# S5 stage of a hybrid decoder: the input factor moved from W to C, W of all quarters and K ahead of the scan

## The chip, the cores and the metric

One core of one Trainium2 chip. The time is the device time of one execution, in microseconds (us). The engines are TensorE (PE in the profile, PEld its weight loads), VectorE (DVE), ScalarE (ACT), GpSimd (POOL) and SyncE (SP), which here issues most DMAs. Each runs its own list of instructions, and they wait for one another through semaphores.

## What is computed

A trunk of two layers on x of 256 tokens by 2048 channels, float32. Layer 0 is an S5 mixer (a complex diagonal state-space model) and a SwiGLU feed-forward; layer 1 is dilated window attention and a second SwiGLU. The change is in the S5 mixer. Its 2048 channels are 128 groups of 16, each with 64 complex states:

```python
lb = exp((lam_re + 1j*lam_im) * dt)              # one factor for each state and group
f = (lb - 1) / (lam_re + 1j*lam_im)              # input factor
bu = einsum('bsgc,gpc->bsgp', u, f * B)          # u = rms_norm(x)
xs[s] = lb * xs[s-1] + bu[s]                     # scan over the 256 tokens
y = real(einsum('bsgp,gcp->bsgc', xs, C)) + d_skip * u
z = gelu(y);  val, gate = split(z @ w_glu);  x = x + val * sigmoid(gate)
```

f depends on state and group alone, so it may stand on B or on C: y is the same.

## The kernel before, in words

**Chunked scan.** The 256 tokens are 64 chunks of 4. Within a chunk everything is matrices: W holds f·lb^(3-j)·B for the four places j of a chunk, V (`vs`) is what each chunk adds to the state (W times u), K (`kt`, spread by DMAs into the Toeplitz blocks `th`) is what the tokens of a chunk do to y directly, and Q (`qp`) holds lb^(t+1)·C, which turns the state at a chunk's start into y. The scan proper then runs over the 64 chunk states in three levels. The groups come as 64 pairs, worked in four quarters of 16 pairs; a half is two quarters, a unit `u` is 8 pairs.

**Steps, with their lines.** `s5_params` (L253) computes lb, its powers `lam`, f (`fx`) and the factors `g` on DVE. `s5_chunk_powers` (L332, POOL) makes lb^4, lb^8 and so on. The loop at L414 scales u by the norm (POOL) and copies it with the halves of the partitions exchanged into `usw` (two SP DMAs a quarter). `w_build` (L445, DVE) makes W of a unit in 12 operations of 256 columns; `v_trans` (L458) transposes it on PE and copies it on ACT (L464); `v_build` (L468) multiplies it by u on PE and copies V on ACT (L479). `k_build` (L483) is 256 small matmuls on W and C, with copies on ACT (L498), and `t_build` (L500) its 16 SP DMAs. `q_build` (L433, POOL) makes Q of a quarter: four complex products, each of three operations on 512 columns (L235 to L237). The scan: `l1` (L532) on DVE or POOL, `l2` (L547) and `l3` (L561) on DVE; `coefs` (L542) copies the chunk powers of a half to PSUM on ACT, for DVE. `t_part` (L579) and `s_part` (L591) are the matmuls for y from th and from the states, with the gelu on ACT; `z_part` (L610) transposes the result for the GLU matmuls.

**Order.** It is written out by hand at L642 to L707, and the framework keeps it: each engine gets its instructions in the order in which the Python code issues them. W is built for units 0 to 5, with V of a unit behind it; then come K of half 0, V of units 4 and 5, Q of quarters 0 and 1 on POOL, and `l1([0, 1])`. The 24 operations of W for units 6 and 7 are strewn into `l2(0)`, V of 6 and 7 follows; `l1([3])` runs on POOL; then `l3(0)`, `s_part(0)`, and so on, with K of half 1 behind `s_part(1)`.

**The stream.** Everything after the mixer is one stream of matmul steps (`stream`, L710): a raw weight tile is loaded by SP, split into two parts (ACT and DVE) and multiplied. Its first eight steps are done unsplit (`plain`, L761; 64 matmuls in all, in blocks of 8) and are placed among the last S5 work by the calls `next(st)`; step 8 is the first ordinary one (L755 to L759). W of quarters 0 to 2 stands in the three buffers of the raw weights, W of quarter 3 in the free ends of `za` and `zb`: weights 0 to 2 can be loaded only when the last reader of that W (`v_trans`, `k_build`) is done.

Of the kernel before, what the change touches and what calls it, by code (L numbers as in the profile page):

```python
# [12 lines left out]
AF = mybir.ActivationFunctionType  # L13
# [87 lines left out]
class Trunk:  # L101
# [39 lines left out]
    def ts(self, out, in0, s1, s2, op0, op1=None):  # L141
        if op1 is None:
            self.nc.vector.tensor_scalar(out, in0, s1, None, op0)
        else:
            self.nc.vector.tensor_scalar(out, in0, s1, s2, op0, op1)
# [107 lines left out]
    def s5_params(self, rms):  # L253
# [45 lines left out]
        kv = lambda v, k: v[:, 0:128 * k].rearrange("p (k r q) -> p k r q", k=k, r=2)  # L299
        nr, fx = ps(192).rearrange("p (r q) -> p r q", r=3), ps(128).rearrange("p (r q) -> p r q", r=2)  # L300
        S3 = [128, 2, 64]
# [9 lines left out]
        nc.vector.tensor_copy(low[:, 0], lam[:, 0, 1:3])  # L311
        ts(nr[:, 0], lam[:, 0, 1], -1.0, None, add)
        ts(nr[:, 2], lam[:, 0, 1], -1.0, 1.0, mul, add)
        nc.vector.tensor_copy(nr[:, 1], lam[:, 0, 2])
        by(lam[:, 1:2, 1:3], low[:, 0], lam[:, 0:1], 1)

        u1, u2 = [v.rearrange("p (r q) -> p r q", r=2) for v in (app, az)]
        tt(u1, bc(lr, S3, [1]), nr[:, 0:2], mul)
        ts(lam[:, 1, 0], lam[:, 1, 2], -1.0, None, mul)
        nc.vector.tensor_copy(low[:, 1], lam[:, 1, 1:3])  # L320
        tt(u2, bc(li, S3, [1]), nr[:, 1:3], mul)
        tt(u1, u1, u2, add)
        by(lam[:, 2:4, 1:3], low[:, 1], lam[:, 0:2], 2)
        tt(fx, u1, bc(dens, S3, [1]), mul)
        ts(lam[:, 2:4, 0], lam[:, 2:4, 2], -1.0, None, mul)
        rms()

        g = self.g = self.bank(7).rearrange("p (j r q) -> p j r q", j=4, r=2)
        nc.vector.tensor_copy(g[:, 3], fx)
        by(g[:, 2::-1], fx, lam[:, 0:3], 3)  # L330

# [30 lines left out]
    def s5(self, st):  # L362
# [32 lines left out]
        r = self.r  # L395
        nc.scalar.activation(bt[:, 2], bt[:, 0], AF.Copy, scale=-1.0)

        def rms():
# [14 lines left out]
        next(powers)  # L413
        for k in range(4):  # L414
            qs = slice(16 * k, 16 * k + 16)
            pool.tensor_tensor(upp[:, qs, :], upp[:, qs, :], bc(rt, [128, 16, 80], [1]), mul)
            nc.sync.dma_start(usw[0:64, qs, :], upp[64:128, qs, 0:64])
            nc.sync.dma_start(usw[64:128, qs, :], upp[0:64, qs, 0:64])
        next(powers, None)
        nc.scalar.activation(ct[:, 0], ct[:, 2], AF.Copy, scale=-1.0)  # L420

# [6 lines left out]

        bq = bt.rearrange("p r (q c) -> p q r c", c=16)
        qv = [self.qp[:, k // 2, 2048 * (k % 2):2048 * (k % 2) + 2048].rearrange("p (r q m) -> p r q m", r=2, q=16)  # L430
              for k in range(4)]

        def q_build(k):  # L433

            qs = slice(16 * k, 16 * k + 16)
            sh = [128, 2, 16, 16]
            v4 = lambda v: v.rearrange("p (r q c) -> p r q c", r=2, q=16)
            for t in range(4):
                self.cmul(pool, qv[k][:, :, :, 16 * t:16 * t + 16], bc(self.lam[:, t, 1, qs], sh, [1, 3]),
                          bc(self.lam[:, t, 2, qs], sh, [1, 3]), ct[:, 1:3, qs], ct[:, 0:2, qs], v4(ptmp[0]), v4(ptmp[1]))  # L440

# [3 lines left out]
        def w_build(k, q0, n):  # L445

            qs = slice(16 * k + q0, 16 * k + q0 + n)
            sh = [128, n, 2, 16]
            w, ops = wt(k, q0, n), []
            for j in range(5):  # L450
                if j < 4:
                    ops += [lambda j=j: tt(w4(t1p[j % 2], n), bc(self.g[:, j, 0, qs], sh, [2, 2]), bq[:, qs, 0:2], mul),
                            lambda j=j: tt(w4(dtmp[j % 2], n), bc(self.g[:, j, 1, qs], sh, [2, 2]), bq[:, qs, 1:3], mul)]
                if j > 0:
                    ops.append(lambda j=j - 1: tt(w[:, :, :, j, :], w4(t1p[j % 2], n), w4(dtmp[j % 2], n), add))
            return ops
# [175 lines left out]

        ws = [self.rawtile() for _ in range(3)] + [(za[:, 3072:4096], zb[:, 3072:4096])]

        def wt(k, q0, n=1):

            w, q0 = (ws[3][q0 // 8], q0 % 8) if k == 3 else (ws[k], q0)
            return w[:, 128 * q0:128 * (q0 + n)].rearrange("p (q r j c) -> p q r j c", q=n, r=2, j=4)

        th = [tz[:, 2048 * h:2048 * h + 2048].rearrange("p (m x) -> p m x", m=4) for h in range(2)]  # L640

        for u in range(6):  # L642
            go(w_build(u // 2, 8 * (u % 2), 8))
            if u < 4:
                v_trans(u, (0, 1))
            if 0 < u < 5:
                v_build(u - 1)
        coefs(0, 5)
        k_build(0, (0, 1))
        t_build(0)  # L650
        for u in (4, 5):
            v_trans(u, (0, 0))
            v_build(u)
        q_build(0)
        q_build(1)
        next(st)
        go(l1([0, 1], dve))
        go(l2(0, self.bank(1)), w_build(3, 0, 8) + w_build(3, 8, 8))
        v_trans(6, (0, 0))
        v_build(6)  # L660
        py = [t_part(0, (1, 7))]
        v_trans(7, (0, 0))
        v_build(7)
        t1p[1] = t1p[0]
        coefs(1, 4)
        q_build(2)
        go(l1([3], pool))

        go(l3(0))
        s_part(0, py[0])  # L670
        py.append(t_part(1, (2, 3)))
        z_part(0, (1, 7), True)
        go(l3(1))
        next(st)
        s_part(1, py[1])
        k_build(1, (0, 5))
        q_build(3)
        next(st)
        t_build(1)
        next(st)  # L680
        z_part(1, (2, 3), True)
        go(l1([2], dve))
        next(st)
        next(st)
        go(l2(1, t1p[0]))
        next(st)
        py.append(t_part(2, (2, 3)))
        next(st)
        go(l3(2))
        s_part(2, py[2])  # L690
        next(st)
        go(l3(3))
# [17 lines left out]
    def stream(self, jobs):  # L710
# [50 lines left out]
        def plain(n, ms):  # L761

            jb, i = steps[n]
            k = jb["ks"][i]
            for m in ms:
                if i == 0:
                    jb.setdefault("ps", {})[m] = [self.bank(b) for b in ((1, 7), (0, 5))[m]]
                for b in range(2):
                    c = 1024 * (n % 2) + 512 * b
                    nc.tensor.matmul(jb["ps"][m][b], self.full(k // 4)[:, k % 4, 128 * m:128 * m + 128],  # L770
                                     raws[n // 2][:, c:c + 512], start=(i == 0), stop=False)
            if n % 2 == 1 and 1 in ms:
                del raws[n // 2]
                load(n // 2 + self.NRAW)

        for u in range(self.NRAW - 1):
            load(u)
        yield
        for n in range(2):
            plain(n, (0,))  # L780
        yield
        load(self.NRAW - 1)
        yield
# [402 lines left out]
```

## Time and profile before

| | us |
|---|---|
| median of 3 runs | 2210.36 (2210.22 to 2210.61) |
| the profiled execution's own time | 2210.46 |
| its span in the profile | 2208.7 |
| PE busy | 2130.2 (96%) |
| DVE busy | 1537.7 (70%) |
| ACT busy | 996.9 (45%) |
| POOL busy | 187.0 (8%) |

Times in the rows are from the start of the span. Idle time of an engine off the bounding chain costs nothing. The S5 stage ends at about 148 us, when step 8 of the stream begins.

### The profile page before, as it was taken

What the parts mean: (1) busy time and instruction counts of PE and PEld (TensorE: products, weight loads), DVE (VectorE), ACT (ScalarE), POOL (GpSimd) and SP (SyncE); (2) the same over time, 40 slices, a digit from 0 to 9 for tenths busy, and PEclk for the clock granted to TensorE, in tenths of its full rate; (3) what the DMA queues carried; (4) which work ended last, traced back from release to release, by engine and by line L of the source; (5) the groups of instructions that cost most, each with busy time, mean ns of one, the idle gap of its engine ahead of it and who ended that gap; (6) DMA issues with size and microseconds to landing.
All of it is one profiled execution on the core that took longest, in us unless ns stands there. A gap on an engine that the chain in (4) does not pass through costs nothing.

```text
span 2208.7 us, 28493 instructions
## 1 busy us (share of the span) xinstructions
PE 2130.2 (96%) x11132; PEld 1753.4 (79%) x11132; DVE 1537.7 (70%) x2656; ACT 996.9 (45%) x1147; POOL 187.0 (8%) x161
## 2 busy tenths in 40 slices
PE   3599999999999999999999999999999999999998
PEld 2468888888888888878888888878888888888886
DVE  8977777677677764756776686687767776774544
ACT  3224445444444443344445555445444444444443
POOL 6820000000000000000000000000000000000000
PEclk9699999999999999999999999999999999999999
DMA  6155555555555555455554454445555555555553
GB/s 180 52 204 191 191 191 209 191 191 191 199 188 188 197 200 192 174 205 181 210 188 150 142 189 152 137 170 191 192 209 191 188 194 190 195 211 204 191 191 133
DMA packets 66838, 404.68 MB, mean 183 GB/s; under 512 B 15248, under 2 KB 16784, under 8 KB 19088
## 3 DMA queue, kind: packets, MB, share of 16 engines
q1 hardware_dynamic: 65696, 397.12, 51.3%
q10 hardware_dynamic: 720, 4.18, 0.5%
q8 instruction: 87, 1.43, 0.3%
q0 software_dynamic: 288, 1.57, 0.2%
q14 instruction: 47, 0.39, 0.0%
HBM read 397.34 MB, written 2.10 MB: 181 GB/s over the span
## 4 chain that ended last, share of the span: by engine, by line
PE 89%; DVE 8%; issue 2%; ACT 1%; DMA 0%; ACTq 0%; DVEq 0%
PE b L756 28%; PE b L759 28%; PE b L755 28%; DVE scr L851 2%; DVE lo L139 1%; PE b L770 1%; PE b L151 1%; DVE b L139 1%; PE b L1074 1%; ACT hi L733 1%; PE b L1105 1%; DVE hi L139 1%; PE b L598 0%; DVE raw L139 0%; PE b L1076 0%
## 5 line engine op out<-in xcount | busy, mean ns | idle before, releaser
L148 DVE SCALAR_TENSOR_TENSOR lo<-raw,gcol,hi 128x1024 fp32r<-128x1024 f32 x464 | 594.6, 1291 | 324.4 <-ACT hi L737 318.5
L755 PE MATMUL b<-hi,xt 128*128 128x512 f32 x1856 | 726.3, 391 | 1.4 <-ACT hi L737 1.4
L756 PE MATMUL b<-lo,xt 128*128 128x512 f32 x1856 | 723.2, 390 | 0.9 <-DVE lo L148 0.9
L737 ACT ACTIVATE hi<-raw,gcol 128x1024 fp32r<-128x1024 f32 x464 | 525.1, 1148 | 399.1 <-PE b L759 378.4
L759 PE MATMUL b<-hi,xt 128*128 128x512 f32 x1856 | 572.1, 389 | 0.0
L139 DVE TENSOR_TENSOR lo<-raw,hi 128x1024 fp32r<-128x1024 f32 x264 | 327.4, 1246 | 288.8 <-ACT hi L733 287.2
L733 ACT CAST hi<-raw 128x1024 fp32r<-128x1024 f32 x264 | 275.0, 1052 | 303.0 <-PE b L759 293.6
L755 PEld LDWEIGHTS b<-hi,xt 128*128 128x128 f32 x1856 | 348.9, 188 | 72.8 <-ACT hi L737 1.8
L759 PEld LDWEIGHTS b<-hi,xt 128*128 128x128 f32 x1856 | 348.6, 188 | 73.1
L756 PEld LDWEIGHTS b<-lo,xt 128*128 128x128 f32 x1856 | 348.9, 188 | 72.6 <-DVE lo L148 1.8
L756 PE MATMUL b<-lo,ht 128*128 128x512 f32 x704 | 274.3, 390 | 2.5 <-DVE lo L139 2.5
L755 PE MATMUL b<-hi,ht 128*128 128x512 f32 x704 | 274.0, 389 | 0.1
L851 DVE STREAM_TRANSPOSE scr<-scr 32x128 f32<-32x128 f32 x704 | 212.9, 302 | 11.3
L759 PE MATMUL b<-hi,ht 128*128 128x512 f32 x704 | 217.2, 389 | 0.0
L756 PEld LDWEIGHTS b<-lo,ht 128*128 128x128 f32 x704 | 132.1, 188 | 31.5 <-DVE lo L139 4.1
L755 PEld LDWEIGHTS b<-hi,ht 128*128 128x128 f32 x704 | 132.1, 188 | 27.7 <-ACT hi L733 0.5
L759 PEld LDWEIGHTS b<-hi,ht 128*128 128x128 f32 x704 | 132.1, 188 | 27.5
L855 POOL TENSOR_TENSOR ht<-scr,ht 128x512 fp32r<-128x512 f32 x44 | 57.0, 1295 | 880.9 <-ACT ht L854 880.9
L854 ACT CAST ht<-scr 128x512 fp32r<-128x512 f32 x44 | 27.3, 621 | 178.3 <-DVE scr L851 178.3
L851 DVE STREAM_TRANSPOSE scr<-x 32x128 f32<-32x128 f32 x320 | 96.8, 302 | 4.9
L855 POOL TENSOR_TENSOR xt<-scr,xt 128x512 fp32r<-128x512 f32 x20 | 25.9, 1296 | 769.6 <-ACT xt L854 641.7
L756 PE MATMUL b<-lo,z 128*128 128x512 f32 x224 | 87.6, 391 | 0.6 <-DVE lo L139 0.6
(196 smaller groups left out, 1454.5 us busy)
## 6 DMA issues: line engine op xcount, KB each, us to landing
raw<-in_fi SPq DMA_DIRECT2D x176, 1024.0 KB, 4.8
raw<-in_fo SPq DMA_DIRECT2D x88, 1024.0 KB, 4.7
raw<-in_wq SPq DMA_DIRECT2D x48, 1024.0 KB, 4.7
raw<-in_glu SPq DMA_DIRECT2D x32, 1024.0 KB, 4.8
raw<-in_wo SPq DMA_DIRECT2D x16, 1024.0 KB, 4.8
raw<-in_kv SPq DMA_DIRECT2D x8, 1024.0 KB, 4.7
xw<-in_xu SPq DMA_DIRECT2D x4, 640.0 KB, 10.3
qp<-in_xr SPq DMA_DIRECT2D x4, 512.0 KB, 9.7
```

The lines of the kernel that those rows point to most:

```text
L139: self.nc.vector.tensor_tensor(out, in0, in1, op)
L148: self.nc.vector.scalar_tensor_tensor(out, in0, s, in1, op0, op1)
L151: self.nc.tensor.transpose(out, in_, self.ident[:n, :n])
L733: nc.scalar.copy(hi, raw)
L737: nc.scalar.activation(hi, raw, AF.Copy, scale=gk)
L755: nc.tensor.matmul(ps[b], xh, hi[:, c], start=first, stop=False)
L756: nc.tensor.matmul(ps[b], xh, lo[:, c], start=False, stop=False)
L759: nc.tensor.matmul(ps[b], xl, hi[:, c], start=False, stop=last)
L770: nc.tensor.matmul(jb["ps"][m][b], self.full(k // 4)[:, k % 4, 128 * m:128 * m + 128], raws[n // 2][:, c:c + 512], start=(i == 0), stop=False)
L851: nc.vector.transpose(out[32 * q:32 * q + 32, :, 32 * a:32 * a + 32], src[32 * a:32 * a + 32, :, q, :])
L854: nc.scalar.copy(dst(0), out)
L855: nc.gpsimd.tensor_tensor(dst(1), out, dst(0).bitcast(F32), ALU.subtract)
```

## The change

f is taken off W and put on C. `s5_params` no longer computes it; `s5_gain` does, on POOL, and `c_gain` multiplies C by it, quarter by quarter, on POOL, with a negated copy on ACT. The last of the four parts of W is then B itself, and is copied by ACT ahead of time; `w_build` makes the other three in 9 operations. The scaling of u is split into two halves, `c_gain` and `q_build` are issued ahead of W, W of all eight units and K of both halves ahead of the scan, W no longer within `l2(0)`. `l1([3])` is issued ahead of `q_build(2)`; some calls of the stream and its PSUM banks move.

```diff
--- before.py
+++ after.py
@@ -297,7 +297,6 @@
         low = ps(256).rearrange("p (k r q) -> p k r q", k=2, r=2)
         t1, t2 = ps(384), ins(384)
         kv = lambda v, k: v[:, 0:128 * k].rearrange("p (k r q) -> p k r q", k=k, r=2)
-        nr, fx = ps(192).rearrange("p (r q) -> p r q", r=3), ps(128).rearrange("p (r q) -> p r q", r=2)
         S3 = [128, 2, 64]
         tt(I(mags), I(mag), I(k2), ALU.bitwise_xor)
 
@@ -309,25 +308,31 @@
         tt(lam[:, 0, 1:3], bc(mags, S3, [1]), pp.rearrange("p (r q) -> p r q", r=2), mul)
         ts(lam[:, 0, 0], lam[:, 0, 2], -1.0, None, mul)
         nc.vector.tensor_copy(low[:, 0], lam[:, 0, 1:3])
-        ts(nr[:, 0], lam[:, 0, 1], -1.0, None, add)
-        ts(nr[:, 2], lam[:, 0, 1], -1.0, 1.0, mul, add)
-        nc.vector.tensor_copy(nr[:, 1], lam[:, 0, 2])
         by(lam[:, 1:2, 1:3], low[:, 0], lam[:, 0:1], 1)
-
-        u1, u2 = [v.rearrange("p (r q) -> p r q", r=2) for v in (app, az)]
-        tt(u1, bc(lr, S3, [1]), nr[:, 0:2], mul)
         ts(lam[:, 1, 0], lam[:, 1, 2], -1.0, None, mul)
         nc.vector.tensor_copy(low[:, 1], lam[:, 1, 1:3])
-        tt(u2, bc(li, S3, [1]), nr[:, 1:3], mul)
-        tt(u1, u1, u2, add)
+        rms()
         by(lam[:, 2:4, 1:3], low[:, 1], lam[:, 0:2], 2)
-        tt(fx, u1, bc(dens, S3, [1]), mul)
+        g = self.g = self.bank(7)[:, 0:384].rearrange("p (k r q) -> p k r q", k=3, r=2)
+        nc.vector.tensor_copy(g, lam[:, 0:3, 1:3])
         ts(lam[:, 2:4, 0], lam[:, 2:4, 2], -1.0, None, mul)
-        rms()
-
-        g = self.g = self.bank(7).rearrange("p (j r q) -> p j r q", j=4, r=2)
-        nc.vector.tensor_copy(g[:, 3], fx)
-        by(g[:, 2::-1], fx, lam[:, 0:3], 3)
+        self.dens = dens
+
+    def s5_gain(self, eng):
+
+        lam, mul = self.lam, ALU.mult
+        lr, li = self.par[:, 0:64], self.par[:, 64:128]
+        nr = self.small(192).rearrange("p (r q) -> p r q", r=3)
+        u1, u2 = [self.small(128).rearrange("p (r q) -> p r q", r=2) for _ in range(2)]
+        f = self.small(128, True).rearrange("p (r q) -> p r q", r=2)
+        eng.tensor_scalar(nr[:, 0], lam[:, 0, 1], -1.0, None, ALU.add)
+        eng.tensor_copy(nr[:, 1], lam[:, 0, 2])
+        eng.tensor_scalar(nr[:, 2], nr[:, 0], -1.0, None, mul)
+        eng.tensor_tensor(u1, bc(lr, [128, 2, 64], [1]), nr[:, 0:2], mul)
+        eng.tensor_tensor(u2, bc(li, [128, 2, 64], [1]), nr[:, 1:3], mul)
+        eng.tensor_tensor(u1, u1, u2, ALU.add)
+        eng.tensor_tensor(f, u1, bc(self.dens, [128, 2, 64], [1]), mul)
+        return f
 
     def s5_chunk_powers(self, eng):
 
@@ -394,6 +399,17 @@
         rt = self.small(80)
         r = self.r
         nc.scalar.activation(bt[:, 2], bt[:, 0], AF.Copy, scale=-1.0)
+        bq = bt.rearrange("p r (q c) -> p q r c", c=16)
+        ws = [self.rawtile() for _ in range(3)] + [(za[:, 3072:4096], zb[:, 3072:4096])]
+
+        def wt(k, q0, n=1):
+
+            w, q0 = (ws[3][q0 // 8], q0 % 8) if k == 3 else (ws[k], q0)
+            return w[:, 128 * q0:128 * (q0 + n)].rearrange("p (q r j c) -> p q r j c", q=n, r=2, j=4)
+
+
+        for u in range(8):
+            nc.scalar.copy(wt(u // 2, 8 * (u % 2), 8)[:, :, :, 3, :], bq[:, 8 * u:8 * u + 8, 0:2])
 
         def rms():
             tt(r, rss[:, :, 0], rss[:, :, 1], add)
@@ -411,12 +427,17 @@
         nc.scalar.copy(rt, psr[:, 0:80])
         powers = self.s5_chunk_powers(pool)
         next(powers)
-        for k in range(4):
+
+        def scale_u(k):
             qs = slice(16 * k, 16 * k + 16)
             pool.tensor_tensor(upp[:, qs, :], upp[:, qs, :], bc(rt, [128, 16, 80], [1]), mul)
             nc.sync.dma_start(usw[0:64, qs, :], upp[64:128, qs, 0:64])
             nc.sync.dma_start(usw[64:128, qs, :], upp[0:64, qs, 0:64])
+
+        scale_u(0)
+        scale_u(1)
         next(powers, None)
+        fx = self.s5_gain(pool)
         nc.scalar.activation(ct[:, 0], ct[:, 2], AF.Copy, scale=-1.0)
 
         ptmp = self.wtile("lo", F32)
@@ -426,18 +447,27 @@
         t1p = [self.bank(6), self.bank(4)]
         cp = self.cp
 
-        bq = bt.rearrange("p r (q c) -> p q r c", c=16)
         qv = [self.qp[:, k // 2, 2048 * (k % 2):2048 * (k % 2) + 2048].rearrange("p (r q m) -> p r q m", r=2, q=16)
               for k in range(4)]
 
-        def q_build(k):
+        def c_mul(o, x, k):
 
             qs = slice(16 * k, 16 * k + 16)
             sh = [128, 2, 16, 16]
             v4 = lambda v: v.rearrange("p (r q c) -> p r q c", r=2, q=16)
+            self.cmul(pool, o, bc(x[:, 0, qs], sh, [1, 3]), bc(x[:, 1, qs], sh, [1, 3]), ct[:, 1:3, qs], ct[:, 0:2, qs],
+                      v4(ptmp[0]), v4(ptmp[1]))
+
+        def c_gain(k):
+
+            qs = slice(16 * k, 16 * k + 16)
+            c_mul(ct[:, 1:3, qs], fx, k)
+            nc.scalar.activation(ct[:, 0, qs], ct[:, 2, qs], AF.Copy, scale=-1.0)
+
+        def q_build(k):
+
             for t in range(4):
-                self.cmul(pool, qv[k][:, :, :, 16 * t:16 * t + 16], bc(self.lam[:, t, 1, qs], sh, [1, 3]),
-                          bc(self.lam[:, t, 2, qs], sh, [1, 3]), ct[:, 1:3, qs], ct[:, 0:2, qs], v4(ptmp[0]), v4(ptmp[1]))
+                c_mul(qv[k][:, :, :, 16 * t:16 * t + 16], self.lam[:, t, 1:3], k)
 
         wT = [self.wtile(w, F32).rearrange("p (q m) -> p q m", q=8) for w in ("hi", "lo")]
         w4 = lambda v, n: v[:, 0:32 * n].rearrange("p (q r c) -> p q r c", r=2, c=16)
@@ -447,10 +477,10 @@
             qs = slice(16 * k + q0, 16 * k + q0 + n)
             sh = [128, n, 2, 16]
             w, ops = wt(k, q0, n), []
-            for j in range(5):
-                if j < 4:
-                    ops += [lambda j=j: tt(w4(t1p[j % 2], n), bc(self.g[:, j, 0, qs], sh, [2, 2]), bq[:, qs, 0:2], mul),
-                            lambda j=j: tt(w4(dtmp[j % 2], n), bc(self.g[:, j, 1, qs], sh, [2, 2]), bq[:, qs, 1:3], mul)]
+            for j in range(4):
+                if j < 3:
+                    ops += [lambda j=j: tt(w4(t1p[j % 2], n), bc(self.g[:, 2 - j, 0, qs], sh, [2, 2]), bq[:, qs, 0:2], mul),
+                            lambda j=j: tt(w4(dtmp[j % 2], n), bc(self.g[:, 2 - j, 1, qs], sh, [2, 2]), bq[:, qs, 1:3], mul)]
                 if j > 0:
                     ops.append(lambda j=j - 1: tt(w[:, :, :, j, :], w4(t1p[j % 2], n), w4(dtmp[j % 2], n), add))
             return ops
@@ -630,65 +660,57 @@
             nc.scalar.copy(hi, full(k))
             pool.tensor_tensor(low, full(k), hi.bitcast(F32), sub)
 
-        ws = [self.rawtile() for _ in range(3)] + [(za[:, 3072:4096], zb[:, 3072:4096])]
-
-        def wt(k, q0, n=1):
-
-            w, q0 = (ws[3][q0 // 8], q0 % 8) if k == 3 else (ws[k], q0)
-            return w[:, 128 * q0:128 * (q0 + n)].rearrange("p (q r j c) -> p q r j c", q=n, r=2, j=4)
-
         th = [tz[:, 2048 * h:2048 * h + 2048].rearrange("p (m x) -> p m x", m=4) for h in range(2)]
-
-        for u in range(6):
-            go(w_build(u // 2, 8 * (u % 2), 8))
-            if u < 4:
-                v_trans(u, (0, 1))
-            if 0 < u < 5:
-                v_build(u - 1)
-        coefs(0, 5)
-        k_build(0, (0, 1))
-        t_build(0)
-        for u in (4, 5):
-            v_trans(u, (0, 0))
-            v_build(u)
+        for k in range(2):
+            c_gain(k)
+        for k in range(2, 4):
+            scale_u(k)
+        for k in range(2, 4):
+            c_gain(k)
         q_build(0)
         q_build(1)
+        for u in range(8):
+            go(w_build(u // 2, 8 * (u % 2), 8))
+            if u == 4:
+                v_build(3)
+                k_build(0, (0, 1))
+                t_build(0)
+                coefs(0, 5)
+            v_trans(u, (0, 1))
+            if u not in (0, 4):
+                v_build(u - 1)
+        v_build(7)
+        k_build(1, (2, 3))
         next(st)
+        t_build(1)
         go(l1([0, 1], dve))
-        go(l2(0, self.bank(1)), w_build(3, 0, 8) + w_build(3, 8, 8))
-        v_trans(6, (0, 0))
-        v_build(6)
-        py = [t_part(0, (1, 7))]
-        v_trans(7, (0, 0))
-        v_build(7)
+        py = [t_part(0, (0, 1))]
+        py.append(t_part(1, (2, 3)))
+        go(l1([3], pool))
+        q_build(2)
+        q_build(3)
+
+        go(l2(0, self.bank(7)))
         t1p[1] = t1p[0]
         coefs(1, 4)
-        q_build(2)
-        go(l1([3], pool))
-
         go(l3(0))
         s_part(0, py[0])
-        py.append(t_part(1, (2, 3)))
-        z_part(0, (1, 7), True)
+        z_part(0, (0, 1), True)
         go(l3(1))
         next(st)
         s_part(1, py[1])
-        k_build(1, (0, 5))
-        q_build(3)
-        next(st)
-        t_build(1)
         next(st)
         z_part(1, (2, 3), True)
         go(l1([2], dve))
         next(st)
         next(st)
+        py.append(t_part(2, (2, 3)))
         go(l2(1, t1p[0]))
         next(st)
-        py.append(t_part(2, (2, 3)))
         next(st)
         go(l3(2))
+        next(st)
         s_part(2, py[2])
-        next(st)
         go(l3(3))
         for i in range(2):
             self.zt[i] = self.ztile(i)
@@ -764,7 +786,7 @@
             k = jb["ks"][i]
             for m in ms:
                 if i == 0:
-                    jb.setdefault("ps", {})[m] = [self.bank(b) for b in ((1, 7), (0, 5))[m]]
+                    jb.setdefault("ps", {})[m] = [self.bank(b) for b in ((0, 1), (7, 5))[m]]
                 for b in range(2):
                     c = 1024 * (n % 2) + 512 * b
                     nc.tensor.matmul(jb["ps"][m][b], self.full(k // 4)[:, k % 4, 128 * m:128 * m + 128],
@@ -773,13 +795,11 @@
                 del raws[n // 2]
                 load(n // 2 + self.NRAW)
 
-        for u in range(self.NRAW - 1):
+        for u in range(self.NRAW):
             load(u)
         yield
         for n in range(2):
             plain(n, (0,))
-        yield
-        load(self.NRAW - 1)
         yield
         for n in range(2):
             plain(n, (1,))
```

## Rows read from the trace of the kernel before

**Rows 1.** page, the chain that ended last, by engine
```profile
PE 89%; DVE 8%; issue 2%; ACT 1%; DMA 0%; ACTq 0%; DVEq 0%
```

**Rows 2.** windows: PE, PEld, DVE, ACT, POOL busy us; PEclk; DMA share; GB/s
```profile
30.00:40.00 10.00, 5.63 (x81) 4.82 (x82) 9.86 (x29) 2.94 (x6) 10.00 (x4) 1.00 0.68 119
...
80.00:90.00 10.00, 4.07 (x104) 3.36 (x96) 9.69 (x33) 1.66 (x3) 5.97 (x6) 0.50 0.01 2
...
180.00:190.00 10.00, 10.00 (x45) 8.27 (x45) 8.03 (x18) 3.74 (x5) 1.30 (x1) 1.00 0.47 170
```

**Rows 3.** chain in order of time: start us, us, what
```profile
93.83 2.15 PE b L598 x128
...
98.44 3.70 PE b L770 x8
...
105.09 1.06 PE b L488 x4
...
113.14 5.83 PE b L770 x8
...
147.79 0.43 PE b L755
```

**Rows 4.** timeline, DVE: start us, us, instruction, [idle before]
```profile
25.34 0.55 DVE L235 TENSOR_TENSOR b<-b,scr 128x384 f32<-128x384 f32 x1
...
27.04 0.43 DVE L139 TENSOR_TENSOR b<-b,z 128x256 f32<-128x256 f32 x1
...
52.42 0.69 DVE L520 TENSOR_TENSOR b<-b,vs 128x512 f32<-128x512 f32 x1
...
66.64 0.42 DVE L139 TENSOR_TENSOR b<-b,z 128x256 f32<-128x256 f32 x1
...
86.16 0.67 DVE L520 TENSOR_TENSOR b<-b,vs 128x480 f32<-128x480 f32 x1
...
101.35 0.70 DVE L520 TENSOR_TENSOR b<-b,vs 128x512 f32<-128x512 f32 x1
...
109.25 0.27 DVE L139 TENSOR_TENSOR b<-b,vs 128x64 f32<-128x64 f32 x1
...
122.50 0.67 DVE L520 TENSOR_TENSOR b<-b,vs 128x480 f32<-128x480 f32 x1
```

**Rows 5.** timeline, POOL
```profile
28.94 11.49 POOL L416 TENSOR_TENSOR xw<-xw,hi 128x1280 f32<-128x1280 f32 x4 [1.84 <-ACT hi L411]
40.38 0.47 POOL L346 TENSOR_TENSOR scr<-scr 128x128 f32<-128x128 f32 x1
...
44.26 1.06 POOL L235 TENSOR_TENSOR lo<-scr,z 128x512 f32<-128x512 f32 x1
...
47.76 1.06 POOL L235 TENSOR_TENSOR lo<-scr,z 128x512 f32<-128x512 f32 x1
```

**Rows 6.** timeline, ACT
```profile
25.26 0.20 ACT L401 ACTIVATE r<-r 128x2 f32<-128x2 f32 x1 [9.61 <-DVE r L145]
...
55.02 0.65 ACT L498 COPY hi<-b 128x256 f32<-128x256 f32 x2 [4.94 <-PE b L493]
...
93.10 1.07 ACT L479 COPY vs<-b 128x512 f32<-128x512 f32 x2 [1.27 <-PE b L475]
94.06 0.50 ACT L545 COPY b<-scr 128x384 f32<-128x384 f32 x1
```

**Rows 7.** timeline, PE
```profile
35.73 1.94 PE L151 MATMUL b<-cst,raw 128*128 128x128 f32 x8 [2.35 <-DVE raw L139]
...
39.96 1.06 PE L151 MATMUL b<-cst,raw 128*128 128x128 f32 x8 [0.61 <-DVE raw L139]
40.96 1.16 PE L475 MATMUL b<-xw,lo 64*64 64x64 f32 x64
...
48.58 1.13 PE L488 MATMUL b<-lo,cst 128*128 128x256 f32 x4
...
62.68 1.99 PE L475 MATMUL b<-xw,lo 64*64 64x64 f32 x64
```

## Prediction

> **What bounds the kernel now.** I read the chain that ended last, then the ten-microsecond windows, then the chain in order of time. By engine the chain is 89% TensorE (PE) [rows 1], but that is an average of two stages. In the windows, VectorE (DVE) is busy 9.7 to 9.9 of 10 us in the S5 stage while PE is busy 4 to 6; later PE is full: at 180 to 190 its 10.00 stand beside 8.03 of DVE [rows 2]. In time, the chain leaves DVE at 93.8, when `s_part(0)` can start, and stays on PE from there: `s_part(0)`, the gelu, the first plain GLU matmuls at 98.44, `k_build(1)` at 105.09, plain matmuls at a slow clock at 113.14, and at 147.79 the first matmul of the ordinary stream (step 8) [rows 3]. After it PE has no slack, so I reduce the question to one number: when does step 8 start? A shift of it moves the end by as much.
>
> **Part 1, DVE before the scan.** Eleven small operations leave `s5_params`, one 384-wide copy comes in. The three 384-wide ones that leave, and a reciprocal, fill 25.34 to 27.04 [rows 4], so about 1.5 us for the three; I estimate the eight of 64 or 128 columns at 0.2 each from the 0.55 of the 384-wide row, and the added copy at 0.5. That is 1.5 + 1.6 - 0.5 = 2.6; I take 2.5 (2.0 to 3.2). W then starts at 24.5 instead of 27.04. A W unit goes from 12 operations to 9, and eight units instead of six stand ahead of the scan: 72 operations as before, which took 52.42 - 27.04 = 25.4 [rows 4]. W is complete at 49.9. The 24 W operations inside `l2(0)` are gone: it ran from 66.64 to 86.16 with them, 19.5, while `l2(1)` without any ran from 109.25 to 122.50, 13.25 [rows 4]; gain 6.3. DVE alone thus becomes 8.8 us shorter up to the end of `l3(0)`. Copying B (eight 256-column copies on ScalarE, ACT, 2.6 us at 0.65 for two [rows 6]) costs nothing: ACT idles 9.61 ahead of the square root at 25.26 [rows 6]; uncovered it would cost its 2.6.
>
> **Part 2, GpSimd (POOL).** Its order is now: half of `scale_u`, the rest of the powers, `s5_gain`, `c_gain(0)`, `c_gain(1)`, the other half of `scale_u`, `c_gain(2)`, `c_gain(3)`, then `q_build`. The first `scale_u` began at 28.94 [rows 5], behind the reciprocal that comes 2.5 earlier: 26.5. Four of them took 11.49 [rows 5], so two take 5.7, to 32.2. The powers took 40.38 to 44.26, 3.9, to 36.1. `s5_gain` is seven operations of 64 or 128 columns; at 0.47 for 128 [rows 5] and fewer for 64, 2.7 (2 to 3.5), to 38.8. A `c_gain` is three operations on 512 columns, the same as one step of `q_build`: 44.26 to 47.76, 3.5 [rows 5]. Two bring 45.8, the other `scale_u` pair 51.5, the last two `c_gain` **58.5**. `q_build(0)` and `(1)` follow, 14 each, to 86.5.
>
> **Part 3, the wait that is added.** Each `c_gain` ends with a small ACT operation (ct[:,0] = -ct[:,2]) that waits for POOL, and all four are issued ahead of the first `v_trans`. ACT takes its instructions in order: `coefs(1,4)`, whose input was ready at 44.3, ran at 94.06, straight behind the copies of `v_build(7)` issued before it at 93.10 [rows 6]. So from about 42 on, ACT stands at these four, and what is queued behind them is everything that carries V: the copies of `v_trans` and `v_build`, of K, and `coefs(0,5)`. PE waits with them, since `v_trans(1)` needs the banks that the copies free; and DVE, done with W at 49.9, waits for V. ACT comes free at 58.5 plus one 256-column operation, 58.9. This is the core of the prediction.
>
> **Part 4, from 58.9 to the scan.** Ahead of `coefs(0,5)`, and so of `l1`, now stand V of units 0 to 3 and K of half 0. Two 512-column copies take 1.07 on ACT [rows 6]; a unit has four. On PE the eight transposes and the 64 matmuls of a unit took 1.06 and 1.16 at 39.96 and 40.96, but 1.94 for transposes at 35.73, and 1.99 for `v_build` at 62.68 [rows 7]. The first pair is the 2.4 GHz level, the slow ones the 1.2 level (0.50 in the window at 80 [rows 2]), although the column says 1.00 at 30 to 40 [rows 2]: durations decide. At 2.4 GHz the units run at 2.8 us (four copies and the hand-overs), `v_build(3)` ends at 69.0; with 1.2 GHz for the first 6 us, which I take since 35.73 also came after idleness, at 71.3; at 1.2 throughout near 75.5. `k_build(0)` took 48.58 to 55.02 [rows 6, 7], 6.4, to 77.7; its copies 0.65 and `coefs` 0.5 bring `l1` to **79** (76.5 at the fast clock alone; 88 at the slow, with K's matmuls doubled). Before, `l1` began at 52.42 [rows 4].
>
> The Trainium skill ("TensorE: Matmul & The Clock Gate", Part 1) says that PE is at the lower clock by default and that sustained activity lifts it. The durations at 35.73 and 39.96 agree, the 1.00 of the column at 30 to 40 does not; by the column alone the sum would be 2221.5, by the rule my 2224.
>
> **Part 5, the scan.** From 79: `l1([0,1])` 14.2 (52.42 to 66.64), `l2(0)` 13.25, `l3(0)` 7.6 (two took 86.16 to 101.35) [rows 4]: 114.0, against 93.7 before. Then `l3(1)` 7.6, `l1([2])` 7.9, `l2(1)` 13.25, two `l3` 15.2 [rows 4]: **157.9**. POOL's `l1([3])` (four steps of 3.5, 14) starts when V of unit 7 is there, about 91.5, and ends at 105.5, ahead of `l2(1)` at 129.5; `q_build(3)` ends at 133.5, ahead of `s_part(3)`. Neither binds.
>
> **Part 6, PE to step 8.** `k_build(1)`, 105.09 to 113.1, and the slow plain block (5.83 against 3.70) [rows 3] leave PE's path: 8.0 + 2.1 = 10.1 gained. PE stood idle before 114.0, so `s_part(0)` is slow, 4 us; gelu and transposes bring the first plain block to 121 (4.6 after the start of `s_part(0)` before [rows 3], now 7). Eight plain blocks at 3.7 and the small parts between them keep PE busy until `l3(2)` at 150.3; then `s_part(2)` 2.0, gelu and transposes 2.0, the last block 3.7: 158.1. `t_part(3)` needs banks 4 and 6, which `l3(3)` holds until 157.9: 1.1, then `s_part(3)` 2.0: step 8 at **161.2**. DVE and PE arrive within half a microsecond, so neither the 8.8 of DVE nor the 10.1 of PE is kept.
>
> SP's edits cost nothing: the `usw` copies of the last two quarters and `t_build(0)` come before loads 0 to 2, `t_build(1)` behind load 2, which waits for `k_build(1)` (about 98). The first reader of those loads is at 121 and that of the second T at 138; without that room each issue would cost about 0.7.
>
> **Sum.** 161.2 - 147.7 = +13.5 on the profiled execution's 2210.46 (0.1 above the median): **2224**.
>
> **Rivals.** *A, ACT is not held.* If ACT were past the negations before V is due, `l1` would wait only for K: `c_gain(1)` at 45.8, `k_build(0)` to 52.3, `l1` at 53.4. Then step 8 comes 25.6 earlier than forecast, less some 1 to 2 us for PE work that no longer hides: about 137, and 2199. For it: the whole saved DVE time of Part 1. Against: the issue order and the 94.06 row. It decides at ACT free by about 45 instead of 58.9, that is `l1` at 65.5. *B, the slow clock stays* through V and K: `l1` at 88, 2233. For it: 0.50 in the window at 80 with PE 4 of 10 busy [rows 2]; against: PE is nearly without gaps at the slow clock here. *C, the wait and the gains cancel*: `l1` near 65, 2210; it needs POOL to be 13 us quicker than its rows.
>
> **Numbers.** Forecast 0.75, B 0.13, A 0.09, C 0.03. The forecast's own bounds (`l1` 76.5 to 82, `s_part(0)` fast or slow) give 2219 to 2228; reaching over to B, and down by the 2 us that the parameter estimates allow, the range is 2217 to 2233. What a measurement can tell is about 0.2%, 4.4 us. Faster 0.09, same 0.03, slower 0.88.
>
> **What would show it.** Right: ACT idle on POOL between about 42 and 58, longest in the list of waits; DVE idle from about 50 to 79, on ACT's `coefs`; first `v_trans` copy at 59; `l3(0)` ending near 114; step 8 near 161. Wrong: `v_trans` copies during W, or `l1` before 65; a first `l1` after 85 would be B.

## The result and the profile after

The changed kernel takes 2223.65 us (median of 4 runs, 2221.65 to 2225.1) against 2210.29 of the kernel before on the same chip; the ratio is 1.0063, 95% interval [1.0048, 1.0078]. It is slower by 13.4 us; forecast was 2224 and slower by 13.5. The execution that was profiled took 2225.1 with a span of 2223.3.

The first thing to read is again who stands longest at whom. These are rows of the list of waits from 20 to 170 us (engine, line, waited for: us in total, times, longest); L465 is the negated copy at the end of `c_gain`, L494 the copies of `v_trans`, L575 `coefs`, L550 the first operation of `l1`.

```profile
ACT xw L634 <- PE b L628: 45.3, 5, 19.9
...
PE b L151 <- ACT hi L494: 30.0, 2, 29.8
ACT z L465 <- POOL z L237: 29.9, 4, 15.1
DVE b L550 <- ACT b L575: 28.8, 1, 28.8
```

ACT waits 29.9 us for POOL at the four negations, PE 30.0 for ACT, DVE 28.8 for ACT: one hold that is handed on twice. The larger sum above them, ACT at the gelu waiting for PE's `s_part`, is five waits and stood in the kernel before too (25.9 in four). Before, PE waited 1.5 us in all for the copies of `v_trans` into this tile, and the other two waits did not occur. The ACT timeline shows the hold itself (start us, us, instruction, idle before):

```profile
42.18 0.42 ACT L465 ACTIVATE z<-z 128x256 f32<-128x256 f32 x1 [15.14 <-POOL z L237]
45.68 0.42 ACT L465 ACTIVATE z<-z 128x256 f32<-128x256 f32 x1 [3.08 <-POOL z L237]
54.74 0.42 ACT L465 ACTIVATE z<-z 128x256 f32<-128x256 f32 x1 [8.64 <-POOL z L237]
58.23 0.42 ACT L465 ACTIVATE z<-z 128x256 f32<-128x256 f32 x1 [3.07 <-POOL z L237]
58.55 1.05 ACT L494 COPY hi<-b 128x512 f32<-128x512 f32 x2
...
78.26 0.50 ACT L575 COPY b<-scr 128x384 f32<-128x384 f32 x1
```

The four negations run at 42.2, 45.7, 54.7 and 58.2, each as POOL has finished its quarter, and the first copy of `v_trans` follows at 58.55. Forecast were "about 42" and 58.9. Before, the copies of V 0 to 3 and K's were done by 55.7 [rows 6], and the scan began at 52.4 [rows 4]. On POOL one sees why:

```profile
26.34 5.74 POOL L433 TENSOR_TENSOR xw<-xw,hi 128x1280 f32<-128x1280 f32 x2
...
35.88 0.37 POOL L328 TENSOR_SCALAR lo<-scr 128x64 f32<-128x64 f32 x1
...
38.73 1.06 POOL L235 TENSOR_TENSOR lo<-scr,z 128x512 f32<-128x512 f32 x1
...
45.61 5.73 POOL L433 TENSOR_TENSOR xw<-xw,hi 128x1280 f32<-128x1280 f32 x2
...
58.28 1.06 POOL L235 TENSOR_TENSOR lo<-scr,z 128x512 f32<-128x512 f32 x1
```

The first half of `scale_u` begins at 26.34 (L433), `s5_gain` at 35.88, `c_gain(0)` at 38.73, the other half of `scale_u` at 45.61, and `q_build(0)` at 58.28, straight behind `c_gain(3)`. The nearest row of before is `scale_u` at 28.94 [rows 5]. DVE:

```profile
24.15 0.41 DVE L139 TENSOR_TENSOR b<-b,z 128x256 f32<-128x256 f32 x1
...
49.23 0.74 DVE L139 TENSOR_TENSOR z<-b,hi 128x256 f32<-128x256 f32 x2
78.79 0.70 DVE L550 TENSOR_TENSOR b<-b,vs 128x512 f32<-128x512 f32 x1 [28.81 <-ACT b L575]
...
106.41 0.67 DVE L550 TENSOR_TENSOR b<-b,vs 128x480 f32<-128x480 f32 x1
...
113.98 0.67 DVE L550 TENSOR_TENSOR b<-b,vs 128x480 f32<-128x480 f32 x1
...
157.72 2.35 DVE L139 TENSOR_TENSOR lo<-raw,hi 128x1024 fp32r<-128x1024 f32 x2
```

W begins at 24.15 instead of 27.04 [rows 4] and ends at 49.97; then DVE stands still for 28.81 us, until `coefs` lets `l1` start at 78.79. `l2(0)` is over at 106.41, `l3(0)` at 113.9, `l3(3)` at 157.7. PE:

```profile
59.17 1.97 PE L151 MATMUL b<-cst,raw 128*128 128x128 f32 x8 [29.82 <-ACT hi L494]
...
66.06 1.09 PE L151 MATMUL b<-cst,raw 128*128 128x128 f32 x8
...
70.61 1.13 PE L518 MATMUL b<-lo,cst 128*128 128x256 f32 x4
...
75.37 2.32 PE L523 MATMUL b<-z,raw 64*64 64x16 f32 x77 [0.85 <-issue]
...
114.09 3.71 PE L628 MATMUL b<-qp,vs 64*64 64x64 f32 x128 [9.61 <-DVE vs L553]
...
120.77 4.86 PE L792 MATMUL b<-raw,xw 128*128 128x512 f32 x8
...
150.54 2.09 PE L628 MATMUL b<-qp,vs 64*64 64x64 f32 x127
153.81 0.27 PE L628 MATMUL b<-qp,vs 64*64 64x64 f32 x1 [1.18 <-issue]
...
162.18 0.50 PE L777 MATMUL b<-hi,z 128*128 128x512 f32 x1
```

Eight transposes take 1.97 at 59.17, after 29.8 us of idleness, and 1.09 at 66.06: the 1.2 and then the 2.4 GHz level, as in [rows 7], while the granted-clock column says 1.00 for 50 to 70 us. `k_build(0)` (L518, L523) runs from 70.61 to 77.7, `s_part(0)` at 114.09 is slow again (3.71 for 128 matmuls, 2.15 in [rows 3]), the first plain block starts at 120.77, and step 8 (L777) at 162.18 instead of 147.7. So `l1` comes 26.4 us later than before, and the stretch from `l1` to step 8 is 11.9 us shorter (95.3 before, 83.4 now): the loss at `l1` is larger than the loss at step 8. Of the 11.9, 6.2 are `l2(0)` without W (13.3 instead of 19.5); K of half 1, which no longer stands behind `s_part(1)`, is the likely rest, but no run takes it apart. From the start of step 8 to the end of the execution it is 2210.46 - 147.72 = 2062.7 before and 2225.1 - 162.18 = 2062.9 after: nothing is lost or won behind step 8, so the start of step 8 tells how much of an execution's time the S5 stage made. On the page the chain by engine has hardly moved from [rows 1], which shows how little an average over the span says here:

```profile
PE 89%; DVE 6%; issue 2%; POOL 1%; ACT 1%; DMA 0%; ACTq 0%; DVEq 0%; POOLq 0%
```

### The profile page after: what moved, and what is told of

It reads as the page before. It is cut to its first block, busy times and chain, and to the rows that moved or that the text cites. A ratio compares the mean times of both kernels' runs of the same rounds, so it can differ in the third digit from the quotient of the medians.

```text
span 2223.3 us, 28491 instructions
## 1 busy us (share of the span) xinstructions
PE 2131.1 (96%) x11132; PEld 1755.9 (79%) x11132; DVE 1528.5 (69%) x2622; ACT 1000.7 (45%) x1159; POOL 203.3 (9%) x180
## 4 chain that ended last, share of the span: by engine, by line
PE 89%; DVE 6%; issue 2%; POOL 1%; ACT 1%; DMA 0%; ACTq 0%; DVEq 0%; POOLq 0%
PE b L778 28%; PE b L781 28%; PE b L777 28%; DVE scr L871 2%; DVE lo L139 1%; PE b L792 1%; PE b L151 1%; PE b L1094 1%; ACT hi L755 1%; PE b L1125 1%; POOL xw L433 1%; PE b L628 0%; PE b L1096 0%; PE b L1095 0%; DVE b L139 0%
## 5 line engine op out<-in xcount | busy, mean ns | idle before, releaser
L777 PE MATMUL b<-hi,xt 128*128 128x512 f32 x1856 | 726.5, 391 | 1.4 <-ACT hi L759 1.4
L777 PEld LDWEIGHTS b<-hi,xt 128*128 128x128 f32 x1856 | 348.8, 188 | 73.4 <-ACT hi L759 1.8
L777 PE MATMUL b<-hi,ht 128*128 128x512 f32 x704 | 274.0, 389 | 0.1
L777 PEld LDWEIGHTS b<-hi,ht 128*128 128x128 f32 x704 | 132.1, 188 | 27.9 <-ACT hi L755 0.5
L875 POOL TENSOR_TENSOR xt<-scr,xt 128x512 fp32r<-128x512 f32 x20 | 25.9, 1294 | 770.1 <-ACT xt L874 642.3
```

The lines of the kernel that those rows point to most:

```text
L777: nc.tensor.matmul(ps[b], xh, hi[:, c], start=first, stop=False)
L875: nc.gpsimd.tensor_tensor(dst(1), out, dst(0).bitcast(F32), ALU.subtract)
```

## The experiments

The theory (H in the texts on record) is that ACT, held by the four negations, holds V and with it the scan. Rival D is that POOL's work has become too long wherever the negations stand; rival P that PE's slow clock and gaps set the price. The summary first; `l1` and step 8 are from each run's profiled execution, medians and ratios from all its runs beside the kernel before. In e4 the profiled execution is not typical: it took 2194.89, 5.8 us less than the median. From step 8 to the end it is 2062.0 to 2063.1 us in every profiled execution but that of e5 (2064.4).

| kernel | `l1` starts | step 8 | median us | ratio to before [95%] |
|---|---|---|---|---|
| before | 52.4 | 147.7 | 2210.29; 2209.39 beside e1 to e4; 2211.06 beside e5 to e7 | 1 |
| changed | 78.8 | 162.2 | 2223.65 | 1.0063 [1.0048, 1.0078] |
| changed, again | 77.2 | 160.5 | 2223.37 | 1.0058 [1.0042, 1.0073] |
| e1, negation on POOL | 55.6 | 139.2 | 2202.41 | 0.9969 [0.9956, 0.9982] |
| e2, negations behind V | 56.9 | 144.0 | 2207.16 | 0.9987 [0.9978, 0.9997] |
| e3, POOL 5 us longer | 84.5 | 168.0 | 2229.42 | 1.0086 [1.0069, 1.0103] |
| e4, K behind V too | 47.6 | 132.9 | 2200.68 | 0.9954 [0.9939, 0.9969] |
| e5, PE kept busy | 77.7 | 161.3 | 2227.35 | 1.0074 [1.0060, 1.0088] |
| e6, K at unit 6 | 49.9 | 135.0 | 2197.06 | 0.9939 [0.9926, 0.9951] |
| e7, POOL in quarters | 46.7 | 132.0 | 2194.01 | 0.9924 [0.9912, 0.9937] |

### e1: the negation on POOL

```diff
-            nc.scalar.activation(ct[:, 0, qs], ct[:, 2, qs], AF.Copy, scale=-1.0)
+            pool.tensor_scalar(ct[:, 0, qs], ct[:, 2, qs], -1.0, None, mul)
```

> The negated copy of C that ends each c_gain is made by POOL instead of ACT; nothing else differs from the changed kernel. Theory H (ACT is held by those four operations, and V with it): ACT copies V during W; k_build(0) waits in PE's order for c_gain(1), about 46.5, so l1 starts near 54 instead of 78.8 and step 8 of the stream near 138 instead of 162.2; time about 2201, some 9 us below the kernel before. Rival D (the work moved to POOL is itself too long): POOL now ends c_gain(3) some 2.5 us later, and the time stays at 2223 or rises to 2226. Rival P (PE's slow clock and idle gaps set the price): a few us at most, 2218 to 2222.

Measured 2202.41; one line turns 0.6% slower into 0.3% faster. Waits in the same stretch:

```profile
ACT hi L494 <- POOL lo L332: 10.6, 1, 10.6
...
DVE b L550 <- ACT b L575: 6.6, 1, 6.6
```

DVE's wait falls from 28.8 to 6.6, `l1` starts at 55.6 and step 8 at 139.2 (54 and 138 expected). POOL got longer, not shorter (the last `c_gain` is over at 60.9 instead of 58.2), and the time fell by 21 us, so D falls; 2218 to 2222, as P had it, did not come either. The 6.6 that are left are the copies of K of half 0, which stand ahead of `coefs` on ACT; e4 takes them away. The upper row is a second new wait that my prediction did not name: the first copy of `v_trans` goes into a buffer that the parameters (`par`) held before, and `s5_gain`, now on POOL, reads lam_re and lam_im there as late as L332. It holds ACT for 10.6 us here; in the changed kernel it hides behind the longer hold.

### e2: the negations behind V

```diff
...
-        q_build(0)
-        q_build(1)
         for u in range(8):
             go(w_build(u // 2, 8 * (u % 2), 8))
...
         v_build(7)
+        for k in range(4):
+            c_neg(k)
+        q_build(0)
+        q_build(1)
         k_build(1, (2, 3))
```

(left out: the negation is taken out of `c_gain` into a function `c_neg`)

> The four negations stay on ACT but are issued behind the copies of V of all units; q_build(0) and q_build(1), which read them, move behind them on POOL. K of half 0 and coefs stand where they stood. Theory H: the same release as with POOL: l1 near 54; q_build(0) starts only at about 64, so POOL's l1([3]) ends near 106 and l2(1) waits some 2 us for it; step 8 near 140, time about 2202. Rival D: no better than 2220, since POOL is no shorter. Rival P: 2218 to 2222.

`l1` is released (56.9; 54 expected), and the time, 2207.16, is 16 us below the changed kernel and 5 above what H gave. The rest is POOL, which now waits for ACT instead:

```profile
PE b L632 <- DVE vs L557: 14.9, 2, 9.9
...
POOL lo L236 <- ACT z L469: 11.6, 1, 11.6
```

```profile
110.77 0.27 DVE L139 TENSOR_TENSOR b<-b,vs 128x64 f32<-128x64 f32 x1 [3.32 <-POOL vs L557]
```

`q_build(0)` stands 11.6 us at a negation (L469) that is now behind all copies of V, POOL's `l1([3])` ends that much later, and `l2(1)` on DVE waits 3.3 us for it at 110.77; PE, which waits 5.0 of the 14.9 us for `l3(2)` in its turn, falls back to the slow clock (`s_part(2)` 3.80 us, 2.09 in e1); the other 9.9 are ahead of `s_part(0)`, as in e1 (9.2). The same engine order that held V when the negations stood ahead holds Q when they stand behind. I had put that wait at 2 us and left out what PE's clock adds.

### e3: POOL made 5 us longer

```diff
+        for i in range(12):
+            pool.memset(ptmp[i % 2], 0.0)
         for k in range(2, 4):
             c_gain(k)
```

> Twelve memsets of a POOL scratch tile (about 5.3 us by the memset of 4096 columns that took 3.51) are put ahead of c_gain(2); they change no result. Theory H: ACT comes free 5.3 us later, l1 starts 5.3 later (84) and the end moves by the whole of it: about 2229 by medians. Rival P: the delay disappears in later gaps of PE, less than 2 us.

The memsets took 5.6 us. `l1` starts at 84.50 and step 8 at 167.96, 5.7 and 5.8 later than in the changed kernel; the median rises by 5.8, to 2229.42. POOL's path ahead of `c_gain(3)` passes into the end in full; nothing later takes it up.

```profile
84.50 0.70 DVE L550 TENSOR_TENSOR b<-b,vs 128x512 f32<-128x512 f32 x1 [34.44 <-ACT b L575]
```

### e4: K of half 0 behind V as well

```diff
             if u == 4:
                 v_build(3)
-                k_build(0, (0, 1))
-                t_build(0)
                 coefs(0, 5)
...
         q_build(1)
+        k_build(0, (0, 1))
+        t_build(0)
         k_build(1, (2, 3))
```

(on top of e2)

> As the kernel with the negations behind V, and K of half 0 with its DMAs also moved behind V of all units; coefs stays in the middle of W. Theory H: nothing ahead of l1 waits for POOL any more; l1 starts as W ends, about 49.7, 29 us earlier than in the changed kernel; POOL's l1([3]) ends near 101 and just meets l2(1); step 8 near 134 and time about 2196 to 2198, 12 to 14 us below the kernel before. If K of half 0 is then too late for t_part(0) (its 16 DMAs end near 75, s_part(0) is due at 85), it would show as PE waiting there. Rival D: 2220 or more.

DVE no longer waits: `l1` starts 0.68 us after W. Step 8 comes at 132.9 (near 134 expected), but in the fastest execution of the four (2194.89); the median, 2200.68, is 3 to 5 us above the 2196 to 2198 expected. Part of the difference is ahead of W: in the profiled execution the parameters were done 2 us earlier than in e1, e2 and e6 (reciprocal at 21.01; 23.14, 22.96, 23.01), for the reason told under e7. Where the other executions of e4 lost the rest was not recorded. What is left shows on PE and DVE:

```profile
47.56 0.70 DVE L554 TENSOR_TENSOR b<-b,vs 128x512 f32<-128x512 f32 x1 [0.68 <-ACT b L579]
...
101.08 0.27 DVE L139 TENSOR_TENSOR b<-b,vs 128x64 f32<-128x64 f32 x1 [2.99 <-POOL vs L557]
```

```profile
77.32 0.44 PE L620 MATMUL b<-tz,xw 64*64 64x64 f32 x2 [2.08 <-DMA tz<-hi]
...
82.78 0.66 PE L632 MATMUL b<-qp,vs 64*64 64x64 f32 x10 [0.39 <-DVE vs L557]
85.45 2.84 PE L632 MATMUL b<-qp,vs 64*64 64x64 f32 x97 [2.02 <-issue]
```

`l2(1)` waits 3.0 for `l1([3])`; `t_part(0)` waits 2.1 for the DMAs of the first T; and `s_part(0)` breaks off for 2.0 us in which PE waits for nothing that the profile shows.

### e5: PE kept busy ahead of `s_part(0)`

```diff
         coefs(1, 4)
+        warm = self.bank(7)
+        for i in range(40):
+            self.tr(warm[:, 128 * (i % 4):128 * (i % 4) + 128], self.ident)
```

(on the changed kernel)

> The changed kernel with forty transposes of a constant put on PE behind l2(0), into a bank that is free there, so that PE works in the gap of 9.6 us ahead of s_part(0); they change no result. s_part(0), 3.7 us, its transposes, 2.0, and the first plain block, 4.9, should take 2.1, 1.0 and 3.7 at the higher clock: 3.7 us less of PE. Theory H (the scan on DVE, which ACT let start late, sets the end): s_part(2) waits for l3(2), which ended at 150.2 as PE came at 150.5, so at most about 1 us is gained, 2222.5 to 2223.7. Rival P (PE's slow clock sets the price): the whole 3.7, 2220 or less.

```profile
105.38 6.22 PE L151 MATMUL b<-cst 128*128 128x128 f32 x40 [3.88 <-DVE vs L139]
113.03 2.10 PE L628 MATMUL b<-qp,vs 64*64 64x64 f32 x128 [1.44 <-DVE vs L553]
...
117.64 3.70 PE L795 MATMUL b<-raw,xw 128*128 128x512 f32 x8 [0.24 <-ACT xw L650]
...
149.33 3.40 PE L628 MATMUL b<-qp,vs 64*64 64x64 f32 x128 [3.00 <-DVE vs L553]
...
161.32 0.50 PE L780 MATMUL b<-hi,z 128*128 128x512 f32 x1
...
165.02 0.50 PE L780 MATMUL b<-hi,z 128*128 128x512 f32 x1 [2.06 <-issue]
```

The clock does rise: `s_part(0)` takes 2.10 instead of 3.71 and the first plain block starts 4.6 us after it instead of 6.7. It buys nothing: PE then waits 3.00 us for `l3(2)` at 149.33, and step 8 is 83.6 us behind the start of `l1`, as in the changed kernel (83.4). Having waited, PE is slow again at `s_part(2)` (3.40; 2.09 in the changed kernel). P falls as the cause. The median is even 4 us above the changed kernel run beside it (2227.35 against 2223.37), which neither theory said. Between the two profiled executions it is 2.4 us: 0.9 ahead of step 8 and 1.5 behind it, where a new gap of 2.06 us stands (165.02) in which PE waits for nothing that the profile shows. Where the rest comes from, and why the extra instructions bring such a gap, stays open.

### e6: K of half 0 and two negations at unit 6

```diff
+            if u == 6:
+                v_build(5)
+                c_neg(0)
+                c_neg(1)
+                q_build(0)
+                q_build(1)
+                k_build(0, (0, 1))
+                t_build(0)
             v_trans(u, (0, 1))
...
```

(on top of e4, from whose end they are taken)

> The version with K behind V, with K of half 0, its DMAs, the first two negations and q_build(0), (1) moved back into the loop at unit 6. POOL's q_build(0) then starts as c_gain(3) ends, 3.8 us earlier, so that l2(1) no longer waits 3.0 for l1([3]); and t_part(0), (1) are done well ahead of s_part(0), which lost 2.0 us to PE's issue. Theory H: l1 as early as before this edit; 1 to 3 us less than the version with K behind V, about 2198 to 2200 by medians, ratio 0.994 to 0.995. If the end is PE's plain blocks alone: no difference.

The median, 2197.06, is 1 us below the 2198 to 2200 expected (the ratio, 0.9939, at their edge), and not for the reason given. DVE's wait ahead of `l2(1)` is gone, yet step 8 is 135.04 - 49.87 = 85.2 us behind `l1`, against 85.4 in e4: the second expectation, that PE's own blocks are the end, holds for this execution. Its chain in order of time says the same: from 53 us to step 8 it runs over PE, with ACT's copies between, and no DVE stands in it. The two versions' intervals overlap (W began 2.0 us earlier in e4's profiled execution than in e6's, so their step 8 is compared from `l1`). `s_part(0)` still breaks off:

```profile
89.01 2.54 PE L632 MATMUL b<-qp,vs 64*64 64x64 f32 x117 [2.55 <-issue]
```

### e7: POOL's scaling of B in quarters

```diff
-        pool.tensor_tensor(bt[:, 0], bt[:, 0], self.gb, mul)
-        pool.tensor_tensor(bt[:, 1], bt[:, 1], ngb, mul)
+        for i, g_ in enumerate((self.gb, ngb)):
+            for e in range(4):
+                c = slice(256 * e, 256 * e + 256)
+                pool.tensor_tensor(bt[:, i, c], bt[:, i, c], g_[:, c], mul)
```

(on top of e6)

> As e6, with POOL's two scalings of B, 1024 columns each and 2.35 us, made in four operations of 256 columns each. In the profiles a DVE operation with one SBUF input and an SBUF output lasted until the end of the POOL operation beside it (4.5 us at 9.71 in the kernel before, 2.4 or none in others). If it waits for the POOL operation as a whole, it now waits at most 0.6 us a time: W starts some 2 to 3 us earlier than in e6's slow cases, the time falls by 1 to 3 us and scatters less. If the long DVE operations have another cause: no difference, or a few tenths more for the smaller operations.

In the changed kernel's timelines the pair looks like this, DVE first, then POOL:

```profile
9.70 4.35 DVE L143 TENSOR_SCALAR hi<-hi 128x64 int32<-128x64 int32 x2
```

```profile
9.35 2.35 POOL L389 TENSOR_TENSOR z<-z,lo 128x1024 f32<-128x1024 f32 x1 [5.09 <-DMA z<-in_bt]
11.65 2.34 POOL L390 TENSOR_TENSOR z<-z 128x1024 f32<-128x1024 f32 x1
```

A DVE shift of 64 columns (two in the row, 4.35 us) ends at 14.05; POOL's second scaling ends at 13.99. In e6 and in e7 (DVE, then POOL) the rows are:

```profile
9.53 2.47 DVE L143 TENSOR_SCALAR hi<-hi 128x64 int32<-128x64 int32 x2
```

```profile
9.31 0.28 DVE L143 TENSOR_SCALAR hi<-hi 128x64 int32<-128x64 int32 x2
...
11.02 0.50 DVE L145 TENSOR_SCALAR hi<-hi 128x64 int32<-128x64 int32 x1
...
12.63 0.26 DVE L145 TENSOR_SCALAR hi<-hi 128x64 f32<-128x64 f32 x1
```

```profile
10.06 2.78 POOL L392 TENSOR_TENSOR z<-z,lo 128x256 f32<-128x256 f32 x4 [5.80 <-DMA z<-in_bt]
```

The median falls by 3.05, to 2194.01, the upper end of the 1 to 3 expected; the scatter did not shrink (3.0 us between the lowest and the highest run in both). That is the fastest version, 0.76% below the kernel before and 1.3% below the changed one. The profile shows the given cause only in part. W starts 2.9 us earlier than in e6 (reciprocal at 20.14 against 23.01), and 2.2 of that is the pair, 0.28 instead of 2.47. But in e7 the pair was over at 9.59, before POOL's first quarter began at 10.06, so the quarters did not shorten it; in e4, with both scalings whole, it was over by their start as well (0.29, ending at 9.87), and W was early too. What the quarters do show is smaller: the next two operations of this kind, which did meet them, took 0.50 and 0.26, against 0.99 and 1.20 beside the whole scalings of e4. How much of the median is the quarters and how much is when POOL's input lands, no run here tells.

## Why the prediction was right

The mechanism was right, and so was the size; that the median lies within 0.4 us of 2224 is partly luck, since single executions ran from 2221.65 to 2225.1 and the profiled one, which the sum describes, is 1.1 above it.

**Part 1** held: W at 24.15 (24.5 forecast), complete at 49.97 (49.9), `l2(0)` without W 13.3 us long. What W gained ahead of the scan was lost to the wait that followed; the earlier parameters reached the end only in that POOL began earlier.

**Part 2** held to 0.3 us: `scale_u` at 26.34 (26.5), `s5_gain` 2.85 long (2.7), `c_gain(3)` done at 58.2 (58.5). These are rows of before multiplied by counts; e3 shows that each microsecond on this path is one at the end.

**Part 3**, the core, is shown and not only argued: the negations stand on ACT where the forecast put them, e1 takes them off and the 23 us of `l1` come back, e3 lengthens the hold and the end follows. What the step missed is the second hold, 10.6 us at the buffer of `par`, which lay inside the first and so cost nothing. One sign was put too strongly: ACT's wait for POOL is not the longest in the list of waits (45.3 at the gelu and PE's 30.0 stand above its 29.9).

**Part 4**: `l1` at 78.8 and, in the second run of the same kernel, 77.2 (79 forecast, 76.5 to 82). That V and K would start at the slow clock was right; the 6 us, an assumption, came out near: transposes still take 1.97 at 62.99 and 1.09 at 66.06. The Trainium skill ("TensorE: Matmul & The Clock Gate", Part 1) has PE at the lower clock after idleness and raised by sustained activity, and the durations agree; the column, 1.00 there, does not show it. `k_build(0)` took 7.1 instead of 6.4, with a gap of 0.85 in it, and began 0.7 earlier than forecast (70.6; 71.3): the two misses cancel, and the 0.2 by which 79 was met is luck. In the second run the last matmuls of K took 1.35 us instead of 2.32, and `l1` came 1.6 earlier.

**Part 5** held to 0.2 us at each step: `l3(0)` over at 113.9 (114.0), `l3(3)` at 157.7 (157.9); POOL's `l1([3])` began at 91.3 (91.5).

**Part 6** was 1.0 short: step 8 at 162.2 for 161.2. `s_part(2)` broke off for 1.18 us ahead of its last matmul (150.54 and 153.81 in the PE rows), a kind of gap that I had not priced, and PE, not the banks of `l3(3)`, was what `t_part(3)` came behind. There is also a slip of counting: of the eight plain blocks seven, not eight, stand ahead of `s_part(2)`, and the last behind it; nothing hangs on it, since the 150.3 of the forecast is the end of `l3(2)`. And its last sentence, that neither gain is kept, goes too far even by its own numbers: `l1` was to come 26.6 later and step 8 only 13.5, so 13.1 were to be made good; 11.9 were. That DVE and PE arrive together is right (150.2 and 150.5 at `s_part(2)`), and e5 confirms that a faster PE alone gains nothing.

**Rival A's** price was about right for the kernel that it described: `l1` at 53.4 and 2199; e1, which comes nearest to it, gives 55.6 and 2202. (Its sum is 2199.8, not 2199: its step 8 at 137 is 10.7 ahead of 147.7.) So the edit does have something to gain: with the hold gone, 7.0 us in e1 and 8.7 in e4, by medians. That this is near the 8.8 of Part 1 does not show that term: in e1 `l1` starts 3.2 us later than before, and the gain is made in the stretch from `l1` to step 8 (83.6 us; 95.3 before). B and C did not occur.

## What to carry to other kernels

When work moves to another engine, look not at the busy time that it adds there but at the small operation that hands the result back: on an engine that works in order, it holds all that is issued behind it until the slow engine is done. Work out when its input is ready, and issue it no earlier in that engine's list than that, or make it on the engine that produces the input. And where such an operation is put later instead, ask who reads it: e2 only moved the wait to POOL.

## What was not expected of the hardware

**DVE and POOL.** A DVE operation with one input and its output in SBUF lasted until the end of the POOL operation beside it: the pair of 64-column shifts took 4.26 to 4.66 us in the kernel before, in both profiles of the changed one, in e3 and in e5, ending within 0.1 us of POOL's second scaling of B; 2.05 to 2.47 in e1, e2 and e6, ending within 0.2 us of the first; and 0.28 to 0.29 in e4 and e7, where it was over by the time the first began. In e1 and e6 the pair began up to 0.1 us ahead of the first scaling, in the long cases 0.04 to 0.43 behind it; e2, 0.45 behind and 2.05 long, does not fit that order. The Trainium skill ("SBUF — State Buffer", section "SBUF: two separate sides") says that DVE in its two-port mode and POOL share a pair of ports, which the first to start keeps for its whole instruction; e7 agrees in that the two operations that met POOL's shorter instructions took 0.50 and 0.26, against 0.99 and 1.20 beside the whole ones in e4. That these DVE operations ran in that mode no row shows, and whether the wait accounts for the 2206 and 2209 to 2212 us among the runs of the kernel before, no run here tells either.

**Gaps on PE.** In runs of matmuls PE stops for 0.7 to 4.2 us while it waits for nothing that the profile shows. The kernel before has such gaps too (1.15 in `k_build(0)`, 1.30 in `k_build(1)`). They are of other size and in other places from version to version: 3.33 and 4.17 in `k_build(1)` of the changed kernel and of e1, 1.18 within `s_part(2)` in the changed kernel, 2.0 and 2.55 within `s_part(0)` in e4 and e6, 2.06 at step 8 in e5. No run here tells what they are.
